# Moving the SBUF tiles of a decoder layer so that matmul operands start on multiples of 128 bytes

## The chip, the core and the metric

The kernel runs on one core of a Trainium2 chip. The metric is the device time of one execution, in microseconds (us), taken as the median of several runs. Inputs and output are in the chip's main memory; the layer is one launch.

## What is computed

One hybrid decoder layer over 256 tokens of width 2048: half a SwiGLU feed-forward, a token mixer, and half of a second SwiGLU feed-forward, each added to the residual stream. Cut to its core:

```
def swiglu(x, w_gate, w_up, w_down):
    return (jax.nn.silu(x @ w_gate) * (x @ w_up)) @ w_down

x = x + 0.5 * swiglu(rms_norm(x, ffn1_norm), ffn1_w_gate, ffn1_w_up, ffn1_w_down)
h = rms_norm(x, mix_norm)
parts = jnp.split(h @ w_in, split_at, axis=-1)     # q, 3 x (k, v), gates, q, k, v
o_nsa = nsa_attention(...)                          # compressed, selected and window branches, gated
o_sb = stick_breaking_attention(q_s, k_s, v_s)
y = jnp.concatenate([rms_norm(o_nsa), rms_norm(o_sb)], axis=-1)
x = x + y @ w_out
x = x + 0.5 * swiglu(rms_norm(x, ffn2_norm), ffn2_w_gate, ffn2_w_up, ffn2_w_down)
```

The widths are D_MODEL = 2048, D_FF = 5632, 8 + 8 heads of 128; all data is float32.

## The kernel before

**Split products.** Every weight block is read as float32 (`w_raw`) and split into two parts: ScalarE rounds it to the type fp32r (`w_hi`, L183), VectorE takes the rest (`w_lo`, L184). Activations are split the same way (`xhi`/`xlo`, `ghi`/`glo`, `yhi`/`ylo`). A product is then three fp32r matmuls into the same accumulator, hi·hi, lo·hi and hi·lo (L235 to L237 in `linear`, L426 to L428 in `pair`). In each, the **stationary** operand is a 128 x 128 piece of the activations, loaded into the array ahead of the matmul, and the **moving** operand is a 128-partition row of 512 weight columns (fewer in a few blocks of `w_in`).

**Stages.** `ffn` runs gate and up of 11 column chunks (the first as two plain products, the other ten in `pair`, which mixes seven-product Strassen steps, for j in 1, 3, 5, with plain steps), then the down product in three parts. `proj` makes the blocks of the mixer's input projection, between which the attention work (small float32 matmuls and transposes) is threaded; then `w_out`, then the second `ffn`. In the Strassen steps VectorE also makes weight differences (`w_t`, L409 to L412), which are split into `t_hi` and `t_lo` and are moving operands too.

**Where tiles lie.** Tiles come from pools, and a tile's place in a partition is the sum of the sizes, each rounded up to 32 bytes, of the tiles allocated before it in its pool, and of the pools below. The order is `cpool` (constants), `wpool` (`w_raw`, `w_hi`, `w_lo`), `xpool` (residual stream `xr`), `spool` (small vectors), `gpool` (`ghi`, `glo`, and later `yhi`, `ylo`), and on top of it the pool of the stage: `fpool1`, then `xmpool` and `mixpool`, then `fpool2`. So a 4-byte constant in `cpool` shifts everything above it by 32 bytes.

In the kernel before the addresses fall out as follows, as offset from a multiple of 128 bytes:

- `w_hi`, `w_lo`, `w_raw`, `xr`, `ident`, the masks `mask_a`, `mask_b` and `mask_c`, `pT`, and the query tile of head group 0 (`qnT` in slot `qn0`): 0
- `xhi`, `xlo`, `ghi`, `glo`, `yhi`, `ylo`, `t_hi`, `t_lo`, `w_t`, the SwiGLU results `g0`, `g1`, and most tiles of the mixer (`kT`, `vS`, `ev`, `oy`, `pm`, the query tile of head group 1): 64
- `usuf`, `nones`, `sel4`, `mask_s` (constants behind `cvalid`): 32

Every wide fp32r matmul thus has its stationary operand 64 bytes off a multiple of 128. Its moving operand is on a multiple where it is `w_hi` or `w_lo`, and 64 bytes off where it is `t_hi` or `t_lo`.

Of the kernel before, what the change touches and what calls it, by code (L numbers as in the profile page):

```python
# [9 lines left out]
F32 = mybir.dt.float32  # L10
F32R = mybir.dt.float32r
BF16 = mybir.dt.bfloat16
I32 = mybir.dt.int32
# [5 lines left out]
P = 128  # L19
D_MODEL = 2048  # L20
SEQ = 256
NT = SEQ // P
# [4 lines left out]
NCH = D_FF // CH  # L27
FF_PARTS = [(0, 4), (4, 8), (8, 11)]
STRASSEN = (1, 3, 5)
CMP_BLOCK = 32  # L30
CMP_STRIDE = 16
CMP_HIDDEN = 256
# [12 lines left out]
def hybrid_layer(ctx: ExitStack, tc: tile.TileContext, d: dict, out: bass.AP):  # L45
    nc = tc.nc

    cpool = ctx.enter_context(tc.tile_pool(name="cpool", bufs=1))
    wpool = ctx.enter_context(tc.tile_pool(name="wpool", bufs=2))
    xpool = ctx.enter_context(tc.tile_pool(name="xpool", bufs=1))  # L50
    spool = ctx.enter_context(tc.tile_pool(name="spool", bufs=2))
# [55 lines left out]
    nc.scalar.preload_act_table_set("silu_and_others")  # L107


    ident = cpool.tile([P, P], F32, tag="ident", name="ident")  # L110
    make_identity(nc, ident)
    ident_bf = cpool.tile([P, P], BF16, tag="identb", name="ident_bf")
# [12 lines left out]
    for t in range(NT):  # L125
        nc.gpsimd.affine_select(out=mask_c[:, t], in_=mask_c[:, t], pattern=[[0, 4], [-CMP_STRIDE, 16]],
                                compare_op=ALU.is_ge, fill=NEG, base=t * P - (CMP_BLOCK - 1),
                                channel_multiplier=1)

    nc.gpsimd.affine_select(out=mask_c[:, 0], in_=mask_c[:, 0], pattern=[[0, 4], [0, 16]], compare_op=ALU.is_ge,  # L130
                            fill=0.0, base=-(CMP_BLOCK - 1), channel_multiplier=1)
    cvalid = cpool.tile([P, 1], F32, tag="cvalid", name="cvalid")
    nc.gpsimd.memset(cvalid, 1.0)
    nc.gpsimd.affine_select(out=cvalid, in_=cvalid, pattern=[[0, 1]], compare_op=ALU.is_ge, fill=0.0,
                            base=-(CMP_BLOCK - 1), channel_multiplier=1)

# [13 lines left out]
    sel4 = cpool.tile([P, 32], F32, tag="sel4", name="sel4")  # L150
    for j in range(4):
        nc.vector.tensor_copy(sel4[32 * j:32 * j + 32, :], ident[32 * j:32 * j + 32, 32 * j:32 * j + 32])
    eps_c = cpool.tile([P, 1], F32, tag="eps", name="eps_c")
    nc.vector.memset(eps_c, EPS)


# [25 lines left out]
    def split(hi, lo, src):  # L182
        nc.scalar.copy(hi, src)  # L183
        nc.vector.tensor_tensor(lo, src, hi.bitcast(F32), op=ALU.subtract)  # L184
# [18 lines left out]
    def pump():  # L203
        for gen in list(lanes):
            step(gen)
# [44 lines left out]
    class Stage:  # L250
# [12 lines left out]
        def width(self, gi):  # L263
            return 4 if not self.sums else 8 if gi in STRASSEN else 6

# [14 lines left out]
        def put_sums(self, gi, src):  # L280
# [3 lines left out]
            for j in range(2):  # L284
                k = 2 * gi + j
                nc.scalar.activation(xf[:, 2 * j:2 * j + 2].rearrange("p a b -> p (a b)"), src[:, j], AF.Copy,
                                     scale=gains[:, self.gain, k:k + 1])
            if gi in STRASSEN:
                nc.vector.tensor_tensor(xf[:, NS3], xf[:, A21], xf[:, A11], op=ALU.subtract)
# [40 lines left out]
    def ffn(st, wg, wu, wd, after, fpool, last_part, groups=None):  # L330
# [24 lines left out]
        def ev(name):  # L355
            return fpool.tile([P, CH], F32, tag=name, name=name)
# [22 lines left out]
        def pair(c):  # L379
# [11 lines left out]
            for j in range(nj):  # L391
                if j in STRASSEN:

# [6 lines left out]
            for j in range(nj):  # L400
# [4 lines left out]
                wlo = wpool.tile([P, 4, CH], F32R, tag="wlo", name="w_lo")  # L405
                if j in STRASSEN:
                    split(whi[:, 1:4], wlo[:, 1:4], raw[:, 1:4])
# [13 lines left out]
                for i, (m, f, s) in enumerate(plan[j]):  # L421
# [7 lines left out]
                    if i % 2 == 1:  # L429
                        pump()  # L430
                if j == max(STRASSEN):
                    s1, v, u = ev("s1"), ev("v"), ev("u")
# [48 lines left out]
    def bg_start():  # L481
        load_xT(0)
        for gi in range(1, KD // 2):
            yield False
            load_xT(gi)
        for c in range(4):
            yield from wait(2)
            load_x(c)
            yield from wait(2)
            st1.square(c)  # L490
        st1.finish()

        nc.scalar.dma_start(pos_i, d["positions"])
        nc.scalar.dma_start(invf, d["inv_freq"].partition_broadcast(P))
        yield from wait(16)
        rotary_angles()

    out_gain = gains[:, 3]
    pos_i = cpool.tile([P, NT], I32, tag="pos_i", name="pos_i")
    invf = cpool.tile([P, 64], F32, tag="invf", name="invf")  # L500

    cs = cpool.tile([P, NT, 64], F32, tag="cos", name="cos_t")
    sn = cpool.tile([P, NT, 64], F32, tag="sin", name="sin_t")

    def rotary_angles():
        pos_f = cpool.tile([P, NT], F32, tag="pos_f", name="pos_f")
        nc.vector.tensor_copy(pos_f, pos_i)
        rot = spool.tile([P, 4, NT, 64], F32, tag="sq", bufs=1, name="rot")
        ang, kk, tt = rot[:, 0], rot[:, 1], rot[:, 2]
        for t in range(NT):  # L510
            nc.vector.tensor_scalar(ang[:, t], invf, pos_f[:, t:t + 1], None, op0=ALU.mult)

        for parts in (TWO_PI, (6.28125, 2.0 * PI - 6.28125)):
            nc.vector.tensor_scalar(kk, ang, 1.0 / (2.0 * PI), MAGIC, op0=ALU.mult, op1=ALU.add)
            nc.vector.tensor_scalar(kk, kk, MAGIC, None, op0=ALU.subtract)
            for part in parts:
                nc.vector.scalar_tensor_tensor(ang, kk, -part, ang, op0=ALU.mult, op1=ALU.add)
        pi32 = 3.1415925
        nc.vector.tensor_scalar(tt, ang, pi32, -pi32, op0=ALU.min, op1=ALU.max)
        nc.scalar.activation(sn, tt, AF.Sin)  # L520
        nc.vector.tensor_scalar(kk, ang, 0.5 * PI, -2.0 * PI, op0=ALU.is_gt, op1=ALU.mult)
        nc.vector.scalar_tensor_tensor(ang, ang, 0.5 * PI, kk, op0=ALU.add, op1=ALU.add)
        nc.vector.tensor_scalar(tt, ang, pi32, -pi32, op0=ALU.min, op1=ALU.max)
        nc.scalar.activation(cs, tt, AF.Sin)
# [15 lines left out]
    mp = mctx.enter_context(tc.tile_pool(name="mixpool", bufs=1, reuse_waits="tile"))  # L540
# [61 lines left out]
    def evac(dst, src, scale):  # L602
        nc.scalar.activation(dst, src, AF.Copy, scale=scale)


    def bg_kcvc(pk):
# [15 lines left out]

        parts = [(ci, la) for ci in range(2) for la in range(0, CMP_BLOCK, 4)]
        w1 = {}
# [11 lines left out]
        for ci in range(2):  # L636
            nm = "kv"[ci]
            posT = mp.tile([P, CMP_BLOCK], F32, tag=f"posT{ci}", name="posT")
            nc.scalar.dma_start(posT, d[f"cmp_{nm}_pos"])
            w2 = mp.tile([P, 2, HD], F32, tag=f"w2{ci}", name="w2")  # L640
            nc.scalar.dma_start(w2, d[f"cmp_{nm}_w2"].rearrange("(c p) n -> p c n", p=P))
            w2s.append(w2)
            bt = mp.tile([P, CMP_BLOCK, 2, 16], F32, tag="pbuf", bufs=2, name="bt")
            bts.append(bt)
# [108 lines left out]


    def bg_gates(pq):
        gate = mp.tile([P, NT, 24], F32, tag="gate", name="gate")
        for t in range(NT):
            gt = gate[:, t]
            evac(gt, pq[t][:, :24], r2[:, t:t + 1])
            nc.vector.tensor_scalar(gt, gt, -1.0, 85.0, op0=ALU.mult, op1=ALU.min)  # L760
            nc.scalar.activation(gt, gt, AF.Exp)
            nc.vector.tensor_scalar(gt, gt, 1.0, None, op0=ALU.add)
            nc.vector.reciprocal(gt, gt)
        have["gate"] = gate
        yield True
# [184 lines left out]
    spawn(bg_kv(proj(2048, CH), 1))  # L950
    pq = proj(2560, 24 + 3 * HD)
    spawn(bg_gates(pq))
    spawn(bg_sbq(pq, 24, 3, 0, "qsA"))
    spawn(bg_qn(proj(0, CH), 0))
# [67 lines left out]
```

## Time and profile before

| | |
|---|---|
| time, median of 3 runs (lowest to highest) | 1891.65 us (1891.46 to 1891.96) |
| the profiled execution: its own time | 1892.9 us |
| its span, first to last instruction | 1891.2 us |
| TensorE busy with matmuls | 1867.9 us, 8,615 instructions |
| weight loads (beside the matmuls) | 1529.0 us, 8,617 instructions |
| VectorE, ScalarE busy | 1309.8 us, 896.3 us |
| bytes moved by DMA | 356.60 MB |

PE is TensorE's matmuls, PEld its weight loads, DVE VectorE, ACT ScalarE. The time of the profiled execution is its span and 1.7 us around it. Matmuls are pipelined: the duration printed for one (some 392 ns for 512 columns) is longer than the distance at which the next one starts (some 229 ns), and the latter sets the time.

### The profile page before, as it was taken

Reading aid. Unit: us, or ns where it says so; the run is one execution under the profiler, and the core shown is the slowest. Engines: PE = TensorE matmul, PEld = TensorE weight load, DVE = VectorE, ACT = ScalarE, POOL = GpSimd, SP = SyncE. Lnnn points to the kernel's source line nnn. Section 1 sums busy time; section 2 is a strip of 40 time slices with the busy share of each in tenths; the row PEclk is TensorE's granted clock in tenths of the full one; section 3 lists DMA queues with packets and bytes.
Section 4 is the critical chain, followed back from the end, with each engine's and each line's share of the span. In section 5 each row is a group of like instructions: output and inputs, shape, how many; then the busy total and the mean of one; then the engine's idle time right before and its main releaser. Section 6 shows DMA issues by size and latency. Waiting matters only on the chain.

```text
span 1891.2 us, 21650 instructions
## 1 busy us (share of the span) xinstructions
PE 1867.9 (99%) x8615; PEld 1529.0 (81%) x8617; DVE 1309.8 (69%) x1331; ACT 896.3 (47%) x902; POOL 5.0 (0%) x23
## 2 busy tenths in 40 slices
PE   7999999999999999999999999999999999999999
PEld 6888888887888888778888878888888887888887
DVE  7888558886468866656655566688647887558864
ACT  7555335553345544335455555454434545335542
POOL 0000000000000000000000000000000000000000
PEclk9999999999999999999999999999999999999999
DMA  8565555565565655664533445655555655555654
GB/s 290 195 206 186 193 190 190 198 201 181 198 222 184 214 192 188 228 215 144 167 112 126 141 135 188 200 190 194 187 197 194 206 184 191 188 194 197 204 192 142
DMA packets 190533, 356.60 MB, mean 189 GB/s; under 512 B 9280, under 2 KB 26592, under 8 KB 190432
## 3 DMA queue, kind: packets, MB, share of 16 engines
q1 hardware_dynamic: 188688, 354.65, 56.7%
q8 instruction: 67, 1.10, 0.3%
q10 hardware_dynamic: 1744, 0.58, 0.1%
q14 instruction: 34, 0.28, 0.0%
HBM read 353.09 MB, written 2.10 MB: 188 GB/s over the span
## 4 chain that ended last, share of the span: by engine, by line
PE 97%; DVE 1%; ACT 1%; DMA 0%; issue 0%; SPq 0%; ACTq 0%
PE m L426 15%; PE m L428 15%; PE m L427 15%; PE down L235 9%; PE down L237 9%; PE down L236 8%; PE in L237 4%; PE in L235 4%; PE in L236 4%; PE wo L235 2%; PE wo L237 2%; PE wo L236 2%; PE gt L343 1%; PE no L836 1%; PE up L237 1%; PE up L235 1%
## 5 line engine op out<-in xcount | busy, mean ns | idle before, releaser
L184 DVE TENSOR_TENSOR w_lo<-w_raw,w_hi 128x2048 fp32r<-128x2048 f32 (+2 forms) x329 | 708.7, 2160 | 364.2 <-ACT w_hi L183 364.0
L183 ACT CAST w_hi<-w_raw 128x2048 fp32r<-128x2048 f32 (+2 forms) x329 | 590.1, 1806 | 639.2 <-PE down L236 243.4
L426 PE MATMUL m<-w_hi,xhi 128*128 128x512 f32 x980 | 386.3, 394 | 0.3 <-ACT w_hi L183 0.3
L427 PE MATMUL m<-w_hi,xlo 128*128 128x512 f32 x980 | 384.1, 392 | 0.0
L428 PE MATMUL m<-w_lo,xhi 128*128 128x512 f32 x980 | 320.5, 392 | 0.0
L235 PE MATMUL down<-w_hi,ghi 128*128 128x512 f32 x704 | 275.8, 394 | 0.0
L236 PE MATMUL down<-w_hi,glo 128*128 128x512 f32 x704 | 275.2, 391 | 0.0
L237 PE MATMUL down<-w_lo,ghi 128*128 128x512 f32 x704 | 262.1, 392 | 0.0
L426 PEld LDWEIGHTS m<-w_hi,xhi 128*128 128x128 f32 x980 | 184.0, 188 | 42.6 <-ACT w_hi L183 2.6
L428 PEld LDWEIGHTS m<-w_lo,xhi 128*128 128x128 f32 x980 | 184.1, 188 | 41.2 <-DVE w_lo L184 0.7
L427 PEld LDWEIGHTS m<-w_hi,xlo 128*128 128x128 f32 x980 | 184.2, 188 | 39.8
L184 DVE TENSOR_TENSOR t_lo<-w_t,t_hi 128x2048 fp32r<-128x2048 f32 x60 | 137.3, 2288 | 48.1 <-ACT t_hi L183 48.1
L183 ACT CAST t_hi<-w_t 128x2048 fp32r<-128x2048 f32 x60 | 114.7, 1911 | 114.0 <-DVE w_t L412 108.8
L237 PEld LDWEIGHTS down<-w_lo,ghi 128*128 128x128 f32 x704 | 131.9, 188 | 29.5
L236 PEld LDWEIGHTS down<-w_hi,glo 128*128 128x128 f32 x704 | 132.3, 188 | 28.3
L235 PEld LDWEIGHTS down<-w_hi,ghi 128*128 128x128 f32 x704 | 132.3, 188 | 27.9
L235 PE MATMUL in<-w_hi,xhi 128*128 128x512 f32 (+3 forms) x384 | 147.0, 383 | 0.0
L236 PE MATMUL in<-w_hi,xlo 128*128 128x512 f32 (+3 forms) x384 | 144.3, 376 | 0.0
L237 PE MATMUL in<-w_lo,xhi 128*128 128x512 f32 (+3 forms) x384 | 142.2, 382 | 1.0 <-DVE w_lo L184 1.0
L409 DVE TENSOR_TENSOR w_t<-w_raw 128x1024 f32<-128x1024 f32 x60 | 73.3, 1222 | 36.6 <-DMA w_raw<-in_ffn_w_gate 36.4
L426 PE MATMUL m<-t_hi,xhi 128*128 128x512 f32 x240 | 94.7, 399 | 1.2 <-ACT t_hi L183 1.2
L427 PE MATMUL m<-t_hi,xlo 128*128 128x512 f32 x240 | 93.0, 392 | 0.0
(245 smaller groups left out, 1806.8 us busy)
## 6 DMA issues: line engine op xcount, KB each, us to landing
w_raw<-in_ffn_w_down SPq DMA_DIRECT2D x88, 1024.0 KB, 5.1
w_raw<-in_ffn_w_gate SPq DMA_DIRECT2D x162, 512.0 KB, 4.8
w_raw<-in_ffn_w_up SPq DMA_DIRECT2D x160, 512.0 KB, 3.9
w_raw<-in_w_in SPq DMA_DIRECT2D x36, 1024.0 KB, 5.1
w_raw<-in_w_out SPq DMA_DIRECT2D x16, 1024.0 KB, 5.1
w_raw<-in_ffn_w_up SPq DMA_DIRECT2D x8, 1024.0 KB, 5.4
w_raw<-in_ffn_w_gate SPq DMA_DIRECT2D x7, 1024.0 KB, 6.0
w<-in_cmp_k_w SPq DMA_DIRECT2D x8, 512.0 KB, 5.7
```

What stands on the lines that cost most here:

```text
L183: nc.scalar.copy(hi, src)
L184: nc.vector.tensor_tensor(lo, src, hi.bitcast(F32), op=ALU.subtract)
L235: nc.tensor.matmul(po[t][:, :n], xhi, whi[:, j], start=s, stop=False)
L236: nc.tensor.matmul(po[t][:, :n], xlo, whi[:, j], start=False, stop=False)
L237: nc.tensor.matmul(po[t][:, :n], xhi, wlo[:, j], start=False, stop=e)
L343: nc.tensor.transpose(pt[:, j * SEQ + t * P:j * SEQ + (t + 1) * P], sg[t][:, (2 * i + j) * P:(2 * i + j + 1) * P], ident)
L409: nc.vector.tensor_tensor(ts[:, 0:2], raw[:, 0:1].to_broadcast([P, 2, CH]), raw[:, 1:4:2], op=ALU.subtract)
L426: nc.tensor.matmul(pm[m], ahi, bhi, start=first, stop=False)
L427: nc.tensor.matmul(pm[m], alo, bhi, start=False, stop=False)
L428: nc.tensor.matmul(pm[m], ahi, blo, start=False, stop=end)
L836: nc.tensor.matmul(po[:, h * HD:(h + 1) * HD], pT[:kn, h * P:(h + 1) * P], vv, start=first and h == 0, stop=True, skip_group_check=True)
```

## The change

Nothing is computed differently. Two tiles that nobody reads or writes are added as pads (256 bytes at the start of what follows `gains` in `cpool`, 320 bytes in `spool`); the two 4-byte constants `cvalid` and `eps_c` become columns of one 128-byte tile; the two 8-byte tiles of the positions are rounded up to 64 bytes; and the tile of the gates gets rows of 32 instead of 24 numbers, of which 24 are used.

```
+PAD_C, PAD_S = 256, 320
...
+    cpool.tile([P, PAD_C // 4], F32, tag="pad", name="pad_c")
+    spool.tile([P, PAD_S // 4], F32, tag="pad", bufs=1, name="pad_s")
...
-    cvalid = cpool.tile([P, 1], F32, tag="cvalid", name="cvalid")
+    small = cpool.tile([P, 32], F32, tag="small", name="small")
+    cvalid = small[:, 0:1]
...
-    eps_c = cpool.tile([P, 1], F32, tag="eps", name="eps_c")
+    eps_c = small[:, 1:2]
...
-    pos_i = cpool.tile([P, NT], I32, tag="pos_i", name="pos_i")
+    pos_i = cpool.tile([P, 16], I32, tag="pos_i", name="pos_i")[:, :NT]
...
-        pos_f = cpool.tile([P, NT], F32, tag="pos_f", name="pos_f")
+        pos_f = cpool.tile([P, 16], F32, tag="pos_f", name="pos_f")[:, :NT]
...
-        gate = mp.tile([P, NT, 24], F32, tag="gate", name="gate")
+        gate = mp.tile([P, NT, 32], F32, tag="gate", name="gate")[:, :, :24]
```

What this does to the addresses: the constants behind `pad_c` move up by 256 bytes; `usuf`, `nones`, `sel4` and `mask_s` by 352, from offset 32 to 0; the weight tiles and `xr` by 384 (three times 128), so that they stay at offset 0; everything from `gpool` up by 704, from offset 64 to 0; the tiles behind the gates by 768, at offset 0 as before. All wide matmuls now have both operands at offset 0. Eighteen small matmuls in the mixer still take a slice that begins 64 bytes into a tile. On all five engines the instructions, their order and their waits are the same in both kernels; only addresses differ.

## Rows read from the trace of the kernel before

**Rows 1.** The page: busy time by engine, and the chain that ended last.

```profile
PE 1867.9 (99%) x8615; PEld 1529.0 (81%) x8617; DVE 1309.8 (69%) x1331; ACT 896.3 (47%) x902; POOL 5.0 (0%) x23
...
PE 97%; DVE 1%; ACT 1%; DMA 0%; issue 0%; SPq 0%; ACTq 0%
```

**Rows 2.** Groups by form, TensorE: line, operands, forms, count | busy us, mean ns | idle.

```profile
L426 PE MATMUL m<-w_hi,xhi 128*128 128x512 f32 x980 | 386.3, 394 | 0.3 <-ACT w_hi L183 0.3
L427 PE MATMUL m<-w_hi,xlo 128*128 128x512 f32 x980 | 384.1, 392 | 0.0
L428 PE MATMUL m<-w_lo,xhi 128*128 128x512 f32 x980 | 320.5, 392 | 0.0
L235 PE MATMUL down<-w_hi,ghi 128*128 128x512 f32 x704 | 275.8, 394 | 0.0
...
L235 PE MATMUL in<-w_hi,xhi 128*128 128x512 f32 x288 | 114.9, 399 | 0.0
...
L426 PE MATMUL m<-t_hi,xhi 128*128 128x512 f32 x240 | 94.7, 399 | 1.2 <-ACT t_hi L183 1.2
L427 PE MATMUL m<-t_hi,xlo 128*128 128x512 f32 x240 | 93.0, 392 | 0.0
L428 PE MATMUL m<-t_lo,xhi 128*128 128x512 f32 x240 | 71.3, 394 | 0.0
L235 PE MATMUL wo<-w_hi,yhi 128*128 128x512 f32 x128 | 51.1, 403 | 0.0
```

**Rows 3.** Timeline, TensorE, a plain step of `pair`: start us, us, engine, line.

```profile
400.20 0.39 PE L426 MATMUL m<-w_hi,xhi 128*128 128x512 f32 x1
...
405.93 0.39 PE L427 MATMUL m<-w_hi,xlo 128*128 128x512 f32 x1
```

**Rows 4.** The same in a Strassen step: six matmuls that move `t_hi`.

```profile
436.61 0.39 PE L426 MATMUL m<-t_hi,xhi 128*128 128x512 f32 x1
...
437.99 0.40 PE L428 MATMUL m<-w_lo,xhi 128*128 128x512 f32 x1
```

**Rows 5.** The tile `ident`: loads of two transposes, duration ns minimum/median/maximum.

```profile
L343 PEld LDWEIGHTS gt<-ident,g x176: 137/140/143, 66.5 to 1830.5; 128*128 128x128 f32 x176
...
L303 PEld LDWEIGHTS xt<-ident,xr x64: 138/139/144, 688.5 to 1173.9; 128*128 128x128 f32 x64
```

**Rows 6.** Timeline: four attention scores of head group 0, and of group 1.

```profile
918.23 1.03 PE L811 MATMUL sc<-kT,qnT 128*128 128x256 f32 x4
...
982.68 1.03 PE L811 MATMUL sc<-kT,qnT 128*128 128x256 f32 x4
```

**Rows 7.** Three bf16 mask matmuls with their loads, then all seven.

```profile
916.67 0.10 PEld L809 LDWEIGHTS <-ident_bf 128*128 128x128 bf16 x1
916.67 0.39 PE L809 MATMUL sc<-mask_b,ident_bf 128*128 128x512 bf16 x1
...
924.63 0.10 PEld L809 LDWEIGHTS <-ident_bf 128*128 128x128 bf16 x1
924.85 0.38 PE L809 MATMUL sc<-mask_b,ident_bf 128*128 128x512 bf16 x1
...
998.55 0.10 PEld L809 LDWEIGHTS <-ident_bf 128*128 128x128 bf16 x1 [0.27 <-issue]
998.56 0.39 PE L809 MATMUL sc<-mask_b,ident_bf 128*128 128x512 bf16 x1
...
L809 PE MATMUL sc<-mask_b,ident_bf x7: 376/379/390, 916.7 to 998.6; 128*128 128x512 bf16 x7
```

**Rows 8.** Groups by form, VectorE and ScalarE: the splits of `w` and `t`.

```profile
L184 DVE TENSOR_TENSOR w_lo<-w_raw,w_hi 128x2048 fp32r<-128x2048 f32 x255 | 582.6, 2290 | 349.6 <-ACT w_hi L183 349.5
L184 DVE TENSOR_TENSOR t_lo<-w_t,t_hi 128x2048 fp32r<-128x2048 f32 x60 | 137.3, 2288 | 48.1 <-ACT t_hi L183 48.1
...
L183 ACT CAST w_hi<-w_raw 128x2048 fp32r<-128x2048 f32 x255 | 485.6, 1911 | 589.9 <-PE down L236 242.1 <-PE m L427 205.8 <-issue 54.3
L183 ACT CAST t_hi<-w_t 128x2048 fp32r<-128x2048 f32 x60 | 114.7, 1911 | 114.0 <-DVE w_t L412 108.8 <-PE m L427 2.5 <-PE m L428 1.4
```

## The prediction

> **What bounds the kernel now.** I read the page's busy table and chain first: TensorE is busy 1867.9 us of a span of 1891.2, and 97% of the chain that ended last is its own [rows 1]. So only what changes the distance between matmuls can move the time by more than a little; VectorE, ScalarE and the DMA queues count where TensorE waits for them, and the chain gives each of them 1% or less.
>
> Next the groups by form, to see what TensorE does. The wide matmuls, fp32r with 512 moving columns, come in the groups of [rows 2]: 980 on each of three lines with `w_hi` or `w_lo` moving, 240 on each of three lines with `t_hi` or `t_lo` moving, and 704, 288 and 128, each standing for three lines with equal counts. That is 3 x (980 + 240 + 704 + 288 + 128) = 7,020 wide matmuls. (The plain first chunks of the feed-forwards hold some more, which I leave out.) The durations printed there overlap, so the pace is read from the timeline: from the start at 400.20 to that at 405.93 stand 25 matmuls, 5.73 us / 25 = 229 ns each [rows 3]. 7,020 x 0.229 = 1,608 us, 85% of the span.
>
> Then the question that decides the case: does anything in this trace depend on whether an operand lies at offset 0 or 64? The kernel before has pairs of like instructions that differ in just that, and the remaining views compare them.
>
> **The change part by part.** No engine gets or loses an instruction or a wait, so every term is a duration times a count. The sum is made against the profiled execution's own time, 1892.9 us (span 1891.2 and 1.7 around it), 1.25 us above the median of 1891.65.
>
> *Moving operand of 720 matmuls from 64 to 0* (`t_hi`, `t_lo`). Here the trace has both cases on the same lines. Moving from 64, L427 has a mean of 392 ns, as it has moving from 0. L428 has 394 against 392, L426 399 against 394 [rows 2]. If all of that were the offset, the gain would be 240 x (5 + 0 + 2) ns = 1.7 us. But the L426 group holds the matmuls that stood first after a wait (1.2 us of idle before it [rows 2]), and the six `t_hi` matmuls between 436.61 and 437.99 start 1.38 / 6 = 230 ns apart [rows 4], with a reading error of a few ns against the 229 above. L427, the line with no waits, is the nearest row: I take 0, and keep -1.7 us as the end.
>
> *Stationary operand of all 7,020 from 64 to 0.* No wide matmul of before has its stationary operand at 0, so this needs bounds. The ends: a bf16 matmul of 512 columns has a median of 379 ns [rows 7] where fp32r has 392 [rows 2]. If the 13 ns between them were all due to the offset, the change would give back 7,020 x 13 ns = 91 us. In the other direction, the same bf16 group reaches 390, 11 ns over its median; if a stationary load at the stream's own offset cost a stream that, the change would add 7,020 x 11 ns = 77 us. The nearest rows lie at 0. The transposes of L303 load from `xr` (offset 0) in a median of 139 ns, where those of L343 load from `g` (offset 64) in 140 [rows 5]. The attention scores (L811) use the same `kT` (offset 64) and the same shapes with queries at offset 0 in head group 0 and at 64 in group 1: four take 1.03 us in both [rows 6]. And the 11 ns of the mask matmuls follow something else. At 916.67 and 924.85 the load that runs during the matmul is of group 0, offset 0, at 998.56 of group 1, offset 64; the durations are 0.39, 0.38 and 0.39. What goes with the longer ones is the matmul's own bf16 load, issued at most 0.01 us ahead at 916.67 and 998.55, and 0.22 us ahead at 924.63 [rows 7]. So I take 0.
>
> *Small matmuls of the mixer.* Some 1,200 records (8,615 less 7,020 and the first chunks' few hundred) hold offsets of 32 or 64 that go to 0. [Rows 5, 6] are such matmuls at both offsets and differ by 1 ns or less: 0, with 1.2 us to either side.
>
> *VectorE and ScalarE.* Writing `t` at offset 64 takes what writing `w` at 0 takes: 2288 against 2290 ns, and 1911 against 1911 [rows 8]. What hides this term anyway is the distance to the matmuls; were the cover gone, 315 splits x 2 ns = 0.6 us. The big DMA targets (`w_raw`, `xr`) stay at offset 0. Term 0.
>
> The sum is 0, and the forecast is the median as it stands, **1891.6 us**.
>
> **The rivals.** *Faster: the offset is what keeps a wide matmul at 229 ns.* For it: bf16 is 13 ns shorter at the same 512 columns, and all wide matmuls share the 64 bytes of their stationary operand, so the trace cannot refute it on the instruction itself. Then 1891.65 - 91 = 1800.6 us, or less of a gain if only a part is due to it; from 0.54 ns each (3.8 us / 7,020) it would be outside no change. Against it: [rows 5, 6], where loads from 0 are no shorter and no kinder to the stream they run beside, and that the load (188 ns or less of busy time each: 1529.0 us / 8,617 is 177 [rows 1]) ends before the 229 ns are over, so that its length is not what the next matmul waits for. The Trainium skill, page "TensorE: Matmul & The Clock Gate", section "Back-to-back issue gap", gives about 216 ns from one start to the next for 512 columns; the trace's 229 [rows 3] stands above it, and by that figure the most to be had here would be 7,020 x 13 ns, the same 91 us. The page names no alignment among its conditions.
>
> *Slower: streams and loads on the same offset get in each other's way.* Before, 6,300 of the 7,020 have the moving operand at 0 and the stationary at 64; after it all have both at 0. The only wide matmuls of before with both at the same offset are the 720 that move `t` (64 and 64). On L428 they take 394 ns against 392 [rows 2]. If those 2 ns come of the equal offsets, 6,300 x 2 ns = 12.6 us are added: 1904.2 us. It decides from 0.6 ns a matmul (3.8 us / 6,300). For it: L428, and the 230 against 229 ns of the starts. Against it: L427, 392 in both, and the scores, whose group 1 has both operands at 64 and whose group 0 has 64 and 0, at the same 1.03 us [rows 6]. The skill's same page, section "Step-by-step: what each phase is for", says that TensorE reads moving data and weights through two independent ports, so that a load takes nothing from the running stream; by it this rival adds 0 us, by L428 12.6. The rows of the scores side with the page, L428 does not, and nothing here has both operands at 0 in a wide matmul.
>
> *The change does not do what it says*: eighteen small matmuls keep an offset of 64. At 13 ns each that is 0.2 us, so this cannot be seen in the time, whichever mechanism holds.
>
> **How the numbers follow.** A measurement of this kernel tells about 0.2%, 3.8 us, from no change; "within" below is 1887.9 to 1895.4. No change has the comparisons of four kinds of rows on its side: 0.76. Faster by more, the full 91 us or a part of it: 0.12. Slower by more, around 12.6 us and less: 0.12. The range covers no change and the weaker part of the slower case, up to about 0.85 ns a matmul (5.4 us), and on the faster side the 1.7 us of the `t` matmuls, the 1.2 us of the small ones and 0.6 us of the splits with what a measurement cannot tell: 1887.0 to 1897.0, which leaves out some 2 in 10.
>
> **What would show it.** In the profile of the changed kernel, if I am right: 25 plain wide matmuls in 5.73 us within 0.02; L427 at 392 ns for `w` and for `t`; four scores in 1.03 us in both groups; the loads of L303 and L343 at 139 to 140; busy TensorE 1867.9 us within 3. If the starts of plain wide matmuls come nearer than 228 ns, the faster rival holds, and if they go past 230, the slower one. If only the `t` matmuls shorten, the time moves by less than 2 us and cannot be told from none. I would be wrong if fp32r loads answer to the offset as loads of transposes and of float32 scores do not, or if equal offsets of both operands matter only at the pace of an fp32r stream, for which the trace has just the `t` matmuls.

## The result: 0.8% faster, through a few nanoseconds on every wide matmul

The changed kernel takes 1877.32 us (median of 4 runs, 1875.95 to 1877.63), the kernel before, measured beside it, 1891.81. The ratio is 0.992, with an interval from 0.990 to 0.994. The forecast was no change, 1891.6 us with a range from 1887.0 to 1897.0; it was wrong. The profiled execution of after took 1877.4 us (span 1875.7), 15.5 us less than that of before in time and in span.

The page of the changed kernel, its busy table and its chain by engine:

```profile
PE 1853.4 (99%) x8615; PEld 1529.2 (82%) x8617; DVE 1308.7 (70%) x1331; ACT 896.6 (48%) x902; POOL 5.0 (0%) x23
...
PE 97%; DVE 1%; ACT 1%; DMA 0%; issue 0%; SPq 0%; ACTq 0%
```

Beside [rows 1], only TensorE's busy time has moved, by 14.5 us; its loads (1529.0 to 1529.2), VectorE (1309.8 to 1308.7) and ScalarE (896.3 to 896.6) are as they were, and so is the chain.

TensorE's groups by form, after (line numbers are 6 higher; columns as in [rows 2]):

```profile
L432 PE MATMUL m<-w_hi,xhi 128*128 128x512 f32 x980 | 383.6, 392 | 0.4 <-ACT w_hi L189 0.4
L433 PE MATMUL m<-w_hi,xlo 128*128 128x512 f32 x980 | 381.5, 389 | 0.0
L434 PE MATMUL m<-w_lo,xhi 128*128 128x512 f32 x980 | 318.5, 390 | 0.0
...
L241 PE MATMUL down<-w_hi,ghi 128*128 128x512 f32 x704 | 273.2, 390 | 0.0
...
L432 PE MATMUL m<-t_hi,xhi 128*128 128x512 f32 x240 | 94.2, 397 | 1.2 <-ACT t_hi L189 1.2
L433 PE MATMUL m<-t_hi,xlo 128*128 128x512 f32 x240 | 92.7, 390 | 0.0
```

The first four of these groups have lost 0.6 to 0.9% of their busy time (386.3 to 383.6 us, 384.1 to 381.5, 320.5 to 318.5, 275.8 to 273.2). Of the other wide groups most lost between 0.2 and 1.5%; one of 64 matmuls, `gate<-w_lo,xhi`, took 0.5 us more (24.9 to 25.4). The pace is read from the timeline again, the same 25 matmuls of the same plain step of `pair` as in [rows 3]:

```profile
396.18 0.39 PE L432 MATMUL m<-w_hi,xhi 128*128 128x512 f32 x1
...
401.84 0.39 PE L433 MATMUL m<-w_hi,xlo 128*128 128x512 f32 x1
```

5.66 us / 25 = 226.4 ns, against 229. Over the whole trace, I took the distance from the start of each fp32r matmul of 512 columns to the start of the next, where that is one of the same kind and less than 250 ns away: 229.4 ns on the mean of 7,138 before, 227.2 ns on that of 7,136 after. 7,136 x 2.2 ns = 15.7 us, the whole of what the span lost. The single distances show more than the mean. Before, they change all the time, mostly between 226, 229 and 232 ns; after, most of them are 227, 227, 226 in turn, that is 226.67 ns. That beat, 226.67 ns, is called *even* below, and every other course of the distances *uneven*. So the question for the experiments was which of the moved addresses makes a stream of wide matmuls even.

### The profile page after: what moved, and what is told of

The parts are those of the page before. It is cut to its first block, busy times and chain, and to the rows that moved or that the text cites. A ratio compares the mean times of both kernels' runs of the same rounds, so it can differ in the third digit from the quotient of the medians.

```text
span 1875.7 us, 21650 instructions
## 1 busy us (share of the span) xinstructions
PE 1853.4 (99%) x8615; PEld 1529.2 (82%) x8617; DVE 1308.7 (70%) x1331; ACT 896.6 (48%) x902; POOL 5.0 (0%) x23
## 4 chain that ended last, share of the span: by engine, by line
PE 97%; DVE 1%; ACT 1%; DMA 0%; issue 0%; SPq 0%; ACTq 0%
PE m L432 15%; PE m L434 15%; PE m L433 15%; PE down L241 9%; PE down L243 9%; PE down L242 8%; PE in L241 4%; PE in L243 4%; PE in L242 4%; PE wo L241 2%; PE wo L242 2%; PE wo L243 2%; PE gt L349 1%; PE no L842 1%; PE up L241 1%; PE up L242 1%
## 5 line engine op out<-in xcount | busy, mean ns | idle before, releaser
L432 PE MATMUL m<-w_hi,xhi 128*128 128x512 f32 x980 | 383.6, 392 | 0.4 <-ACT w_hi L189 0.4
L433 PE MATMUL m<-w_hi,xlo 128*128 128x512 f32 x980 | 381.5, 389 | 0.0
L434 PE MATMUL m<-w_lo,xhi 128*128 128x512 f32 x980 | 318.5, 390 | 0.0
L241 PE MATMUL down<-w_hi,ghi 128*128 128x512 f32 x704 | 273.2, 390 | 0.0
L189 ACT CAST t_hi<-w_t 128x2048 fp32r<-128x2048 f32 x60 | 114.7, 1912 | 117.8 <-DVE w_t L418 112.9
```

What stands on the lines that cost most here:

```text
L241: nc.tensor.matmul(po[t][:, :n], xhi, whi[:, j], start=s, stop=False)
L432: nc.tensor.matmul(pm[m], ahi, bhi, start=first, stop=False)
L433: nc.tensor.matmul(pm[m], alo, bhi, start=False, stop=False)
L434: nc.tensor.matmul(pm[m], ahi, blo, start=False, stop=end)
```

## The experiments

**What was on trial.** Measured modulo 512, the operands of the wide matmuls lie as follows. Before: `w` at 128, the stationary tiles and `t` at 320. After: all at 0. Three theories fit the result. **S**: a stationary operand that is 64 bytes off a multiple of 128 is slow to load beside a stream. **M**: the place of the moving operand counts. **R**: neither place counts, but how far the stationary operand lies behind the moving one, the *difference* below; modulo 256 it was 192 before and is 0 after. Beside them stands what the change says: that operands on a multiple of 128 bytes are fast. All kernels but the three of bare matmuls compute the whole layer, with the same instructions; their edits only set where tiles lie.

**One operand off at a time.** Three kernels change the two pads of the changed kernel.

```
k1_st64     PAD_C, PAD_S = 256, 384    # moving 0,  stationary 64, difference 64
k2_mv64     PAD_C, PAD_S = 320, 256    # moving 64, stationary 0,  difference 192
k3_both64   PAD_C, PAD_S = 320, 320    # moving 64, stationary 64, difference 0
```

> The changed kernel with 64 bytes more of pad in spool: the stationary operands of all wide matmuls go back to offset 64 (and t_hi, t_lo as moving operands with them), w_hi and w_lo stay at 0. Theory S (the stationary operand's offset alone costs the 2.2 ns a wide matmul): 1892 us, plain wide matmuls 229 ns apart. Theory R (what counts is that moving and stationary operand lie at different offsets): 1892 us as well. Theory M (the moving operand's offset counts): 1877 us but for the 720 t matmuls, at most 2 us more. A theory that only multiples of 512 bytes count gives 1892 us too, and is told apart by a later run.

> The changed kernel with 64 bytes of pad moved from spool to cpool: w_hi and w_lo, the moving operands, lie at offset 64, all stationary operands at 0, t_hi and t_lo at 0. Theory S: 1877 us, wide matmuls 227 ns apart. Theory R (unequal offsets): 1892 us. Theory M: 1892 us or more. DMA targets w_raw and xr also move to 64; if that costs, TensorE's waits at its start grow, not the distance of the matmuls.

> The changed kernel with 64 bytes more of pad in cpool: moving and stationary operands of all 7,404 wide matmuls lie at offset 64. Theory S: 1892 us. Theory R (unequal offsets): 1877 us. Theory M: 1892 us. If moving and stationary each cost 2 ns: 1907 us.

Measured: k1_st64 1918.0 us, ratio 1.014 [1.012, 1.015]; k2_mv64 1892.5 us, 1.000 [0.9995, 1.001]; k3_both64 1877.6 us, 0.992 [0.991, 0.994]. S falls: with the stationary operand on a multiple of 128 (k2) nothing is gained, and with it off (k3) all is gained. M falls with the same two, the other way round. What the two fast kernels share is a difference of 0. And k1 shows more than that: a difference of 64 is not like 192 but much worse. R as it stood on record, equal or unequal offsets, had 1892 us for k1 and missed by 26 us; from here on R means that the size of the difference decides. The same groups in k1_st64, and a plain step of 25 wide matmuls of its timeline:

```profile
L432 PE MATMUL m<-w_hi,xhi 128*128 128x512 f32 x980 | 388.5, 397 | 0.3
L433 PE MATMUL m<-w_hi,xlo 128*128 128x512 f32 x980 | 386.5, 395 | 0.0
```

```profile
405.46 0.39 PE L432 MATMUL m<-w_hi,xhi 128*128 128x512 f32 x1
...
411.29 0.39 PE L433 MATMUL m<-w_hi,xlo 128*128 128x512 f32 x1
```

5.83 us / 25 = 233.2 ns, 6.8 more than after.

**The price by offset, with nothing else running.** A kernel of stages of 64 matmuls each, that reads `x` and computes nothing of the reference.

```
for k in range(R):                                    # R = 64
    a = s // size + 128 * (k % 2)                     # s, m: offsets in bytes
    b = m // size
    nc.tensor.matmul(po[:, :n], w[:, a:a + P], v[:, b:b + n], start=k == 0, stop=k == R - 1)
```

> Not the layer: x alone is read, and TensorE runs 39 stages of 64 matmuls each, with nothing beside them; a stage has one pair of offsets (moving, stationary) for fp32r of 512, 384 or 256 columns, or bf16 of 512. Theory S: in fp32r of 512 columns the stages with the stationary operand at 0 or 128 (mod 128) take 64 x 227 ns = 14.5 us, those at 64 take 14.7 us, whatever the moving offset. Theory R: stages with equal offsets 14.5 us, others 14.7. bf16 stages: 13.8 us at every offset. If VectorE's and ScalarE's traffic is needed for the difference, all stages of a kind are equal here.

Its timeline, one row a stage (start us, duration us of the 64 together):

```profile
25.55 14.67 PE L60 MATMUL stab<-mv,st 128*128 128x512 f32 x64
40.05 14.68 PE L60 MATMUL stac<-mv,st 128*128 128x512 f32 x64
54.57 15.09 PE L60 MATMUL stad<-mv,st 128*128 128x512 f32 x64
69.49 15.10 PE L60 MATMUL stae<-mv,st 128*128 128x512 f32 x64
...
99.41 15.04 PE L60 MATMUL stag<-mv,st 128*128 128x512 f32 x64
...
129.22 14.82 PE L60 MATMUL stai<-mv,st 128*128 128x512 f32 x64
143.88 14.67 PE L60 MATMUL staj<-mv,st 128*128 128x512 f32 x64
...
217.35 15.30 PE L60 MATMUL stao<-mv,st 128*128 128x512 f32 x64
...
262.24 14.81 PE L60 MATMUL star<-mv,st 128*128 128x512 f32 x64
...
395.23 14.70 PE L60 MATMUL stba<-mv,st 128*128 128x512 f32 x64
...
467.94 14.81 PE L60 MATMUL stbf<-mv,st 128*128 128x512 f32 x64
482.59 14.68 PE L60 MATMUL stbg<-mv,st 128*128 128x512 f32 x64
497.11 15.10 PE L60 MATMUL stbh<-mv,st 128*128 128x512 f32 x64
512.05 7.82 PE L60 MATMUL stbi<-mv,st 128*128 128x256 f32 x64
519.70 7.70 PE L60 MATMUL stbj<-mv,st 128*128 128x256 f32 x64
...
605.94 13.99 PE L60 MATMUL stbs<-mb,sb 128*128 128x512 bf16 x62
```

A stage holds 63 distances and the duration of its last matmul (0.39 us for fp32r with 512 columns, 0.34 with 384 and 0.28 with 256), so a row of 14.67 is (14.67 - 0.39) / 63 = 226.7 ns a matmul:

| stage | moving, stationary | difference mod 256 | ns |
|---|---|---|---|
| stab | 0, 0 | 0 | 226.7 |
| stac | 0, 16 | 16 | 226.8 |
| stad | 0, 32 | 32 | 233.3 |
| stae | 0, 64 | 64 | 233.5 |
| stag | 0, 128 | 128 | 232.5 |
| stai | 0, 192 | 192 | 229.0 |
| staj | 0, 256 | 0 | 226.7 |
| stao | 4, 0 | 252 | 236.7 |
| star | 64, 0 | 192 | 228.9 |
| stba | 64, 64 | 0 | 227.1 |
| stbf | 128, 320 (as before) | 192 | 228.9 |
| stbg | 64, 320 | 0 | 226.8 |
| stbh | 64, 128 | 64 | 233.5 |

No other engine works here, so VectorE and ScalarE have no part in it, and the numbers are those of the layer: 229 for before, 233 for k1. Where the offsets are multiples of 32, the difference modulo 256 sorts the rows to within some 1 ns; a place by itself does not (stationary at 64: 233.5 with the moving operand at 0, 227.1 with it at 64). With finer offsets the place has a part after all: stao, difference 252 by a moving operand at 4, ran at 236.7 ns, and 252 by a stationary operand at 252 runs at 226.7 or 233 (the last kernel below). In the layer all tiles lie on multiples of 32. A bf16 matmul of 512 columns stands at 216 ns at all four pairs of offsets tried (stbs is the first; two of its 64 records are missing). An fp32r matmul of 256 columns even likes the difference of 64 better (stbi 119.7 at 0, stbj 117.8 at 64).

**Multiples of 128, and the change in parts.** Three kernels for the theory that the change itself states, and for its parts.

```
k4_st128    PAD_C, PAD_S = 256, 448      # after: moving 0, stationary 128
k5_spad64   + spool.tile([P, 16], F32, tag="pad", bufs=1, name="pad_s")     # to the kernel before, nothing else
k6_onlyc    - spool.tile([P, PAD_S // 4], F32, tag="pad", bufs=1, name="pad_s")   # from after
```

> The changed kernel with the state pool's pad at 448 instead of 320 bytes: the moving tiles stay at 0, the stationary tiles come to 128 (mod 512), t too. Every operand is then on a multiple of 128 bytes, and the difference (stationary minus moving) is 128 (mod 256). Theory 'multiple of 128' (what the change says): as the changed kernel, 1877 us. Theory R (the difference modulo 256 decides): m1_offsets has 232.3 to 232.5 ns at a difference of 128, 5.7 ns over 226.7; times some 6,700 matmuls that is 38 us, so 1915 us (1908 to 1920), slower than before.

> The kernel before with one line more: a pad of 64 bytes ahead of the state pool's tiles. The moving tiles stay at 128, the stationary tiles go from 320 to 384 (mod 512): the difference becomes 256, that is 0 modulo 256. Nothing else of the change is in it. Theory R: all of the gain, 1877 us (1875 to 1879). If the constants' pad, the rounded small tiles or the moving tiles' own place had a part in it, more than 1880.

> The changed kernel without the state pool's pad; the constants' pad and the rounded tiles stay. Moving tiles at 0, stationary tiles at 192: the difference is 192, as in the kernel before. Theory R: no gain, 1892 us (1890 to 1894). If the constants' pad or the rounding carried part of the gain, less than 1889.

Measured: k4_st128 1912.8 us, ratio 1.011 [1.009, 1.012]; k5_spad64 1876.2 us, 0.992 [0.990, 0.993]; k6_onlyc 1892.1 us, 1.000 [0.999, 1.001]. TensorE's busy time on the pages of k4_st128 and k5_spad64:

```profile
PE 1888.5 (99%) x8617; PEld 1529.9 (80%) x8617; DVE 1311.1 (69%) x1331; ACT 895.9 (47%) x902; POOL 5.0 (0%) x23
```

```profile
PE 1851.7 (99%) x8617; PEld 1527.5 (81%) x8617; DVE 1308.9 (70%) x1331; ACT 896.3 (48%) x902; POOL 5.1 (0%) x23
```

So the stated reason does not hold: k4 has both wide operands on multiples of 128 bytes, and is 21 us slower than the kernel before, by 20.6 us of matmul time. And one pad of 64 bytes in the kernel before is worth as much as the whole change. The pad of the constants, the rounded tiles and the gates' rows are worth nothing here (k6).

**Small differences, narrow loads, short runs.** A second kernel of bare stages, as above; it computes nothing of the reference.

> Stages of 64 matmuls with a float32r operand pair, nothing else running; it computes nothing of the reference. (1) Differences in steps of 4 bytes: R expects 226.7 ns where the difference is 16 bytes or less (m1_offsets has it at 16) and 228 to 237 ns else. (2) A stationary operand of 64 and of 32 columns at difference 0: if the load takes time from the stream (the 32 cycles above 512 in 226.7 ns are its 128 columns), 220 and 216.7 ns; if it takes none, 226.7 at either. With 384 and 256 moving columns and 64 stationary columns: 166.7 and 113.3 ns against 173.3 and 120. (3) Runs in turn: 12 matmuls at difference 192 and then 4 at difference 0, as the t tiles stand among the w tiles in the kernel before: if a stream needs some matmuls to settle, as the first 5 to 11 of a stage in m1_offsets, the 4 stand 229 to 233 ns apart, else 226.7. 12 at (0, 0) and 4 at (256, 256), all of difference 0: 226.7 throughout.

```profile
85.03 15.09 PE L58 MATMUL staf<-mv,st 128*128 128x512 f32 x64
...
204.03 14.88 PE L58 MATMUL stan<-mv,st 128*64 128x512 f32 x64
218.75 14.99 PE L58 MATMUL stao<-mv,st 128*32 128x512 f32 x64
...
277.76 11.26 PE L58 MATMUL stas<-mv,st 128*64 128x384 f32 x64
288.85 7.44 PE L58 MATMUL stat<-mv,st 128*64 128x256 f32 x64
296.12 14.83 PE L58 MATMUL stau<-mv,st 128*128 128x512 f32 x64
310.79 14.88 PE L58 MATMUL stav<-mv,st 128*128 128x512 f32 x64
325.50 14.87 PE L58 MATMUL staw<-mv,st 128*128 128x512 f32 x64
340.21 14.67 PE L58 MATMUL stax<-mv,st 128*128 128x512 f32 x64
354.71 14.68 PE L58 MATMUL stay<-mv,st 128*128 128x512 f32 x64
```

*Short runs.* stau is the pair of before, difference 192; stax is the pair of its `t` tiles, difference 0: 229.2 against 226.7 ns. In stav 12 matmuls of the former and 4 of the latter take turns, as in a Strassen step of before, and the row is no shorter than stau's: 4 matmuls at difference 0 gain nothing among others. In staw there are 12 at difference 0 to 4, and that is no shorter either. In stay two pairs of places that are both at difference 0 take turns, and it runs like stax. *Small differences.* Here I had expected too much, 226.7 ns up to a difference of 16: staf, difference 16, takes 233.3 ns, where m1_offsets had it at 226.8 (stac), and the stages at 4, 8 and 12 take 232.4, 230.6 and 229.9. *Narrow loads.* The stationary operand of 64 columns brings the wide stream to 230 ns (stan) and that of 32 to 231.7 (stao), not to the 220 and 216.7 that I expected if the load took time from the stream in proportion. With 384 moving columns and 64 stationary ones it is 173.3 ns (stas), as with 128 stationary columns, and not 166.7. Only with 256 moving columns does the half load give what was expected, 113.3 ns once the stage has settled (stat; 120.0 with 128 columns).

**Why 16 came out twice.** In m1_offsets the stage at 16 followed an even one, in m2_offsets an uneven one. Two more kernels were to settle whether that is the reason, one of bare matmuls (nothing of the reference) and one of the layer.

```
k7_spad80   + spool.tile([P, 20], F32, tag="pad", bufs=1, name="pad_s")     # to before: meant for difference 16, gives 32
m3_settle   ahead of each stage 32 matmuls at difference 0, or 32 at difference 64
```

> As k5_spad64, but with a pad of 80 instead of 64 bytes: the stationary tiles lie 272 bytes behind the moving tiles (mod 512), that is a difference of 16 (mod 256). m1_offsets showed 226.7 ns at 16 in a stage that followed an evenly running one, m2_offsets 233.3 ns in a stage that followed an uneven one. If 16 is as good as 0: 1877 us. If 16 only keeps an even stream even and cannot bring one about, the stream is lost at the first of the some 180 breaks (waits, other tiles) and doesn't come back: 233 ns, 6 above 226.7 in some 6,700 matmuls, 1916 us (1905 to 1920). If a break loses it only for a while: between.

> Stages of 64 matmuls at one difference each, and ahead of each 32 matmuls either at difference 0 (even) or at 64 (uneven); nothing else runs, it computes nothing of the reference. If the state in which a stage begins counts: a difference of 0 runs at 226.7 ns from either start (after some 4 to 12 matmuls from the uneven one), 16 at 226.7 ns from the even and 233 ns from the uneven start, all others at 228 to 237 ns from either. If only the difference counts: the same mean from both starts at each difference.

```profile
25.72 14.67 PE L51 MATMUL stac<-mv,st 128*128 128x512 f32 x64
...
47.69 14.70 PE L51 MATMUL stae<-mv,st 128*128 128x512 f32 x64
...
69.48 15.04 PE L51 MATMUL stag<-mv,st 128*128 128x512 f32 x64
...
202.40 14.67 PE L51 MATMUL stas<-mv,st 128*128 128x512 f32 x64
...
224.38 15.09 PE L51 MATMUL stau<-mv,st 128*128 128x512 f32 x64
...
557.39 14.67 PE L51 MATMUL stby<-mv,st 128*128 128x512 f32 x64
...
579.36 15.10 PE L51 MATMUL stca<-mv,st 128*128 128x512 f32 x64
```

stac and stae are difference 0 after an even and after an uneven run: 14.67 and 14.70. From the uneven one the starts stand 231, 231, 235, 229, 232, 231 ns apart and then 227, 226, 227 to the end. stas and stau are difference 16: even (226.7) from the even run, 233.3 from the uneven one, to the end of the stage in both. stby and stca, difference 252 (that is -4), do the same; so do 12, 240 and 244 (240 stands at 228.3 in its uneven form), while stag, difference 4, loses the even beat at once, as 8, 20, 236 and all farther ones did. My expectation had only 16 keep it. So, with the moving operand at 0, difference 0 is the one of the thirteen that *brings about* the even stream; a few others near it only keep one. That is the reason why 16 came out twice.

k7_spad80 took 1917.4 us, ratio 1.013 [1.012, 1.015]. That lies in the range expected of 16, but by luck, for the kernel doesn't have a difference of 16. A tile's size is rounded up to 32 bytes, so the pad of 80 takes 96: the stationary tiles lie at 416 modulo 512, and the difference is 32. Its trace fits this: 235 and 232 ns are the most frequent of its distances (4,555 of 7,141), as in the bare stage at 32 (stad in m1_offsets, 233.3 ns), while the uneven stage at 16 (staf in m2_offsets) has every second distance at 233 ns. So k7_spad80 gives the layer's time at a difference of 32. What the layer would make of 16, which bare matmuls keep even but don't bring about, stays open.

## Why the prediction was wrong, step by step

**What bounds the kernel: right.** TensorE was the bound, its distance between wide matmuls was what could move the time, and nothing else did.

**The stationary operand: the step that failed.** It was set at 0 between -13 and +11 ns a matmul; 2.2 ns were gained. The ends held; the choice between them was made by "the nearest rows", and these were near in the wrong respect. Loads of transposes, float32 scores and bf16 mask matmuls [rows 5 to 7] have like operands at both offsets and do not answer to them, and they still don't after (the loads of L309 and L349 have a median of 140 ns, four scores take 1.02 to 1.03 us). But m1_offsets shows that type and width decide: bf16 of 512 columns does not answer at all, fp32r of 256 answers the other way. (Float32 was not run bare; that the transposes and scores stayed silent because of their type is argued.) And the rows were sorted by the offset of one operand, where the relation between the two counts. A comparison on other types had no say on fp32r with 512 columns, and the prediction's last sentence, that fp32r might answer "as loads of transposes and of float32 scores do not", named the gap without giving it a chance of its size.

**The `t` matmuls: a right reading of rows that could not show it.** They alone had both operands at one place before, and stood 230 ns apart [rows 4]. That was taken as evidence that a common place is worth nothing, and by the slower rival as 2 ns of cost. But they stand in short runs, mostly of four or eight and at most of twelve, among `w` matmuls at difference 192, and stav shows that a run of four does not settle (runs of eight were not tried by themselves). After, where all have difference 0, `t_lo` matmuls stand 226.7 ns apart (143 distances), 231.6 before.

**The faster rival** had the right direction, and the mark that was to show it is there: starts nearer than 228 ns. Its mechanism, the offset of the stationary operand itself, falls with k2 and k3. Nor were the 13 ns from bf16 to fp32r to be had at any of the places tried: bf16 is at 216 ns at all of its four, and fp32r at 226.7 at the best. The Trainium skill, page "TensorE: Matmul & The Clock Gate", section "Back-to-back issue gap", gives that 216 as the gap of an isolated matmul and some 131 ns for a sustained stream of loads and matmuls. The bf16 stages here ran at the 216, no fp32r stream reached it, and none of either type came near 131.

**The slower rival** looked at the right thing, the two operands' relation, with the wrong sign: equal places are the best case, not the worst. Relations that cost do exist, and cost more than its 12.6 us: the differences 128 and 64 of k4 and k1 lost 21 and 26 us to the kernel before. By the Trainium skill's page "TensorE: Matmul & The Clock Gate", section "Step-by-step: what each phase is for", the load of the next weights takes no read bandwidth from the running matmul. The runs here do not bear out that the two are independent: the same loads and streams take 226.7 to 233.5 ns by where their operands lie to each other.

**The other terms.** The splits, the small matmuls and the eighteen left at 64 were right at 0: VectorE's and ScalarE's busy times are within 1.1 us, and the 256-column matmuls of the input projection (96 of them) grew by some 3 to 4 ns each, 0.3 us. How the lower end of the range, 1887.0, is added up from its four terms is not clear (in a plain sum they give 1884.3), but the measured 1877.3 lies below either.

**What is left of the gain.** The even beat is 226.67 ns, the mean after is 227.2. Counted from each break in the trace of after, the first ten distances have means of 227 to 233 ns and the eleventh and later ones 226.7. With some 110 such runs of wide matmuls that is the 0.5 ns x 7,136 = 3.6 us which the breaks still cost. No kernel beat the changed one by more than the runs scatter; the kernel before with one pad of 64 bytes equals it.

## What to carry to other kernels

Where fp32r matmuls with 512 columns run back to back, put the stationary and the moving tiles a multiple of 256 bytes apart; a pad of one tile does it (its size is rounded up to 32 bytes, so work out the address), and the alignment of either by itself was worth nothing here. Any change to a pool below them may move the difference: between the best and the worst place lay 41 us in 1,877 (k1_st64 against the changed kernel), so look at it whenever an edit that should be neutral isn't. And in a trace look at the single distances, not only their mean: a beat that wanders (226, 229, 232) where each instruction does the same work is a hint that a better place may exist. A regular beat is no proof that there is none: in the step of k1_st64 shown above the distances are 233, 233, 234 ns in turn, and that is among the slowest.

## What the runs showed of the hardware

- An fp32r stream of 512 columns with a load of 128 x 128 for each has a pace that depends on (stationary address - moving address) modulo 256: 226.7 ns at 0, 233.3 at 32, 233.5 at 64, 232.5 at 128, 229.0 at 192; in the layer 1877, 1917, 1918, 1913 and 1892 us. This holds for places on multiples of 32 bytes (128 came out at 232.4 and 233.3); with the moving operand 4 bytes off, the place counted too.
- At the same difference a stream can run in more than one form. At difference 0 it falls into the even one within some 11 matmuls of a start or a break. With the moving operand at 0, a stream at 12, 16, 240, 244 or 252 keeps an even one that it is given and does not find it by itself; with the moving operand at 4, 252 lost the even one at once (236.7 ns).
- Even paces at difference 0 were 226.7 ns for 512 columns, 173.3 for 384 and 120.0 for 256; at 2.4 GHz, the level at which the clock was granted in these stages (mean granted clock 0.996 of full in m1_offsets), that is 544, 416 and 288 cycles, 32 above the number of columns each time. A load of half as many columns took 256 columns to 113.3 ns, 16 above. This fits with a load that takes cycles from the stream, a quarter of a cycle for each of its columns; but 512 columns with the half load ran at 230 ns and not at 220, 384 at 173.3 and not at 166.7, and 256 columns with the whole load but a difference of 64 at 117.8 ns, under their 288 cycles. So it is a guess that these stages speak against. What it is that repeats every 256 bytes stays open too.
